# Grouped-query stage of a two-block transformer layer: the projection run to its end first, then scores of two pieces together

## The chip, the cores and the metric

One core of a Trainium2 chip. The metric is device microseconds of one execution, median of the runs.

## What is computed

A hybrid layer (differential attention, gated convolution, memory attention, MLP), then two DiT blocks with modulation. The change lies in the first DiT block's attention: 256 tokens, 16 query heads of 64 over 4 key/value heads, fp32.

```python
qkv = h @ w_qkv
q, k, v = jnp.split(qkv, [Q_WIDTH, Q_WIDTH + KV_WIDTH], axis=-1)
q = apply_rope(rmsnorm(q.reshape(B, T, N_HEADS, HEAD_DIM), q_g), cos, sin)
k = apply_rope(rmsnorm(k.reshape(B, T, N_KV_HEADS, HEAD_DIM), k_g), cos, sin)
...
s = jnp.einsum('bqkgd,bskd->bkgqs', q_blk, k).astype(jnp.float32) * scale
p = jax.nn.softmax(s, axis=-1).astype(v.dtype)
return jnp.einsum('bkgqs,bskd->bqkgd', p, v)
...
return o @ w_o
```

## The kernel before

Every weight is split into a high part (`whi`, cast on ScalarE, L90) and a low part (`wlo`, subtraction on VectorE, L91), so that a product of the large matrices is three TensorE passes (`mm3`, L411 to L414). The class `Weights` keeps the plan of all weights in order of use: it loads 1 MB blocks into three raw buffers from SP's queue, splits them into halves of 128x1024 ahead of use (`pump`), bounded by `W.cap`, and defers each low half a little (`rest`, `get`). The program is written in the order in which each engine executes it; nothing reorders it. Small steps between the large products are put off by ticks: `later(n, f)` runs f n ticks on, and `tick` is called after each unit of weights. Each engine takes its list in order, and waits on semaphores.

The grouped-query stage has three projections of 512 columns: keys and values together, the first half of the queries (heads 0 to 7), the second half. Each is four units of weights, 12 products for each of two token tiles. `gemm_cols_skew` does the first two, `gemm_cols` the third. What comes out is normed and rotated: `evac_kv2` and `evac_q2(n)` take sums of squares (`group_ss`: ScalarE squares, VectorE sums), an inverse root by three Newton steps on GpSimd (`rsqrt`, L276), the rotation on VectorE (`rope`), and turn the result by TensorE (`transpose4`, copied by ScalarE into `kT2`, `qT2`). Queries are turned unnormed; their root `rsq2` enters as the scale of the exponentials.

Then come eight pieces of two heads. Of each: `gq_scores` (four products into two PSUM banks, maxima `nm` and `bias` on VectorE), `gq_exp` (four exponentials with sums, ScalarE), `gq_norm` (reciprocal and division, VectorE), `gq_turn` (eight transposes, one bank copied by ScalarE, one by VectorE), `gq_out` (products with v, then `split_to`: cast `omT` on ScalarE and low half on VectorE). `Rows("o2", 8)` multiplies each output by w_o. `gq_pieces` (L1316) lists which steps of which pieces stand together:

```python
for stage in ((gq_scores, 0, None, 0), (gq_turn, 1, gq_exp, 0), (gq_out, 2, gq_norm, 0)):
```

and `piece` (L1332) runs the next of them, raises `W.cap` by one and pumps. `rows.run` calls it between token tiles for the first two outputs, the loop around it for the rest. At k == 2 the cap falls and two steps of the modulation (`ada`, gate lines L1036) are caught up.

## Time and profile before

| | us |
|---|---|
| median of 3 runs | 1311.92 (1311.72 to 1311.97) |
| the profiled execution | 1312.45 |
| its span, first to last instruction | 1310.7 |
| TensorE products busy in it | 1274.4 (97%) |
| VectorE, ScalarE, GpSimd busy | 931.5, 726.1, 132.5 |

The profile is one execution. Times in its rows are microseconds from the start of the span. PE is TensorE, DVE VectorE, ACT ScalarE, POOL GpSimd; a row names the line, the operation, output and input tiles, and in brackets how long the engine was idle before it and what released it. Rows of TensorE overlap in their ends, so distances are read from start to start.

### The profile page before, as it was taken

The numbers are of one execution on the slowest core, as the hardware profiler recorded it, in microseconds if no ns is written. First come the engines' busy times: TensorE is split into PE (matmuls) and PEld (weight loads), VectorE is DVE, ScalarE is ACT, GpSimd is POOL, SyncE is SP. The second block draws the span as 40 slices with busy tenths as digits, with TensorE's granted clock in tenths as the row PEclk, the third lists the DMA queues.
The fourth block names the chain that finished last, engine by engine and source line by source line (L and its number), as shares of the span: only waits on it lengthen the run. The fifth ranks groups of instructions, "written<-read, shape, count | busy, mean of one in ns | idle before, by whom it ended". The sixth has DMA issues, their size and how long they took to land.

```text
span 1310.7 us, 20502 instructions
## 1 busy us (share of the span) xinstructions
PE 1274.4 (97%) x7891; PEld 1117.4 (85%) x7891; DVE 931.5 (71%) x1435; ACT 726.1 (55%) x1177; POOL 132.5 (10%) x345
## 2 busy tenths in 40 slices
PE   8999999999999999999788999999999999999998
PEld 7788789999998989977556899987889988799896
DVE  5746778856787777777776687776888877764453
ACT  6865666544445645445555666445656543684451
POOL 1222253600001000100400000000000000000000
PEclk9999999999999999999989999999999999999999
DMA  7662344557884888984332588885886765465650
GB/s 249 222 225 98 129 161 162 161 193 238 282 276 153 264 286 292 289 304 157 105 110 65 180 295 283 278 313 164 289 283 221 262 232 194 129 224 191 222 193 33
DMA packets 166990, 275.43 MB, mean 210 GB/s; under 512 B 8444, under 2 KB 95276, under 8 KB 166764
## 3 DMA queue, kind: packets, MB, share of 16 engines
q1 hardware_dynamic: 137292, 219.78, 49.9%
q10 hardware_dynamic: 27808, 50.41, 11.6%
q0 software_dynamic: 1792, 3.92, 1.2%
q8 instruction: 62, 1.02, 0.3%
q14 instruction: 36, 0.29, 0.1%
HBM read 273.04 MB, written 1.05 MB: 209 GB/s over the span
## 4 chain that ended last, share of the span: by engine, by line
PE 72%; DVE 10%; DMA 9%; ACT 5%; POOL 2%; issue 2%; ACTq 0%; SPq 0%; DVEq 0%; POOLq 0%
PE bank L412 12%; PE bank L413 12%; PE bank L414 12%; PE bank L512 9%; PE bank L514 9%; PE bank L513 9%; DMA araw<-in_ada_w_dram 5%; DVE wlo L91 3%; PE bank L462 2%; ACT whi L90 1%; DMA raw<-in_w_mem_kv_dram 1%; DMA raw<-in_attn_w_qkv_dram 1%; ACT p L1288 1%; PE bank L1435 1%; PE bank L453 1%
## 5 line engine op out<-in xcount | busy, mean ns | idle before, releaser
L90 ACT CAST whi<-raw 128x1024 fp32r<-128x1024 f32 x411 | 425.2, 1052 | 265.2 <-PE bank L414 64.5
L91 DVE TENSOR_TENSOR wlo<-raw,whi 128x1024 fp32r<-128x1024 f32 x412 | 495.7, 1219 | 85.3 <-ACT whi L90 83.8
L512 PE MATMUL bank<-hT,whi 128*128 128x256 f32 x1152 | 324.9, 282 | 0.0
L513 PE MATMUL bank<-hT,whi 128*128 128x256 f32 x1152 | 321.5, 279 | 0.0
L514 PE MATMUL bank<-hT,wlo 128*128 128x256 f32 x1152 | 321.4, 279 | 0.0
L512 PEld LDWEIGHTS bank<-hT,whi 128*128 128x128 f32 x1152 | 217.1, 188 | 1.9 <-issue 1.3
L514 PEld LDWEIGHTS bank<-hT,wlo 128*128 128x128 f32 x1152 | 218.2, 189 | 0.0
L513 PEld LDWEIGHTS bank<-hT,whi 128*128 128x128 f32 x1152 | 216.6, 188 | 0.6
L413 PE MATMUL bank<-wlo,act 128*128 128x512 f32 x384 | 150.0, 391 | 2.9 <-DVE wlo L91 2.9
L412 PE MATMUL bank<-whi,act 128*128 128x512 f32 x384 | 150.1, 391 | 0.0
L414 PE MATMUL bank<-whi,act 128*128 128x512 f32 x384 | 149.6, 390 | 0.0
L412 PE MATMUL bank<-whi,hT 128*128 128x512 f32 x308 | 126.4, 410 | 0.8 <-ACT hT L336 0.8
L414 PE MATMUL bank<-whi,hT 128*128 128x512 f32 x308 | 121.1, 393 | 0.0
L413 PE MATMUL bank<-wlo,hT 128*128 128x512 f32 x308 | 120.7, 392 | 0.3 <-DVE wlo L91 0.3
L1036 DVE SCALAR_TENSOR_TENSOR acc<-araw,cond,acc 128x512 f32<-128x512 f32 x128 | 95.4, 746 | 32.3 <-DMA araw<-in_ada_w_dram 32.1
L413 PEld LDWEIGHTS bank<-wlo,act 128*128 128x128 f32 x384 | 72.1, 188 | 18.9 <-DVE wlo L91 4.6
L414 PEld LDWEIGHTS bank<-whi,act 128*128 128x128 f32 x384 | 72.1, 188 | 14.9
L412 PEld LDWEIGHTS bank<-whi,act 128*128 128x128 f32 x384 | 72.1, 188 | 14.5
L412 PEld LDWEIGHTS bank<-whi,hT 128*128 128x128 f32 x308 | 57.9, 188 | 17.5 <-ACT hT L336 4.2
L414 PEld LDWEIGHTS bank<-whi,hT 128*128 128x128 f32 x308 | 57.9, 188 | 13.8 <-DVE hT L325 1.0
L413 PEld LDWEIGHTS bank<-wlo,hT 128*128 128x128 f32 x308 | 58.0, 188 | 12.9 <-DVE wlo L91 0.8
L293 DVE TENSOR_TENSOR act<-s,act 128x512 fp32r<-128x512 f32 x36 | 24.9, 691 | 49.7 <-ACT act L292 49.7
(299 smaller groups left out, 1861.2 us busy)
## 6 DMA issues: line engine op xcount, KB each, us to landing
araw<-in_ada_w_dram ACTq DMA_DIRECT2D x192, 256.0 KB
raw<-in_w_in_dram SPq DMA_DIRECT2D x40, 1024.0 KB
raw<-in_mlp_w_in_dram SPq DMA_DIRECT2D x32, 1024.0 KB
raw<-in_mlp_w_out_dram SPq DMA_DIRECT2D x32, 1024.0 KB
raw<-in_gmlp_w_in_dram SPq DMA_DIRECT2D x24, 1024.0 KB
raw<-in_w_mlp_in_dram SPq DMA_DIRECT2D x16, 1024.0 KB
raw<-in_w_mlp_out_dram SPq DMA_DIRECT2D x16, 1024.0 KB
raw<-in_gmlp_w_out_dram SPq DMA_DIRECT2D x12, 1024.0 KB
```

What stands on the lines that cost most here:

```text
L90: self.nc.scalar.copy(hv, v)
L91: self.rests.append(lambda v=v, hv=hv, lv=lv: self.nc.vector.tensor_sub(lv, v, hv.bitcast(F32)))
L293: V.tensor_sub(lo, src, hi.bitcast(F32))
L412: T.matmul(acc, xh, wh, start=start, stop=False)
L413: T.matmul(acc, xh, wl, start=False, stop=False)
L414: T.matmul(acc, xl, wh, start=False, stop=stop)
L453: T.matmul(acc[c][0], act[0][:, k, 0:P], w[1][:, j, :], start=False, stop=(k == 7))
L462: T.matmul(acc[c][0], act[e][:, k, 0:P], w[0][:, j, :], start=(k + e == 0), stop=False)
L512: T.matmul(acc[:, j], wh[:, k, :], act[0][:, k, :], start=(k == 0), stop=False)
L513: T.matmul(acc[:, j], wh[:, k, :], act[1][:, k, :], start=False, stop=False)
L514: T.matmul(acc[:, j], wl[:, k, :], act[0][:, k, :], start=False, stop=(k == 7))
L1036: V.scalar_tensor_tensor(acc, ada_st.pop(j), cond[:, k:k + 1], acc, op0=ALU.mult, op1=ALU.add)
```

## The change

The change adds `rsqrt_v`, the inverse root as a chain of 11 operations on VectorE, and uses it for the keys and for the first half of the queries; the second half stays on GpSimd. The keys are turned together, one unit of weights later. The third projection runs to its end before q's first half is turned; then the scores and exponentials of pieces 0 and 1 are issued together. The second half of q is squared by ScalarE behind these exponentials and rotated directly from PSUM in two parts, its turn comes after output 0's products, and its sums and root after that. Twelve products of `ones` stand on TensorE behind the first scores. From then on a step issues: scores of piece k+3, products of output k, exponentials of k+3, division of k+2, weight split, output k+1, turn of k+2, split of output k+1.

```diff
--- before.py
+++ after.py
@@ -288,6 +288,19 @@
             E.tensor_scalar(u, u, -1.0, 1.5, op0=ALU.mult, op1=ALU.add)
             E.tensor_mul(y, u, y)
 
+    def rsqrt_v(ss, inv, y):
+
+        shape = list(ss.shape)
+        tag = "x".join(map(str, shape[1:]))
+        h = small.tile(shape, F32, tag=f"rh{tag}", name="rh", bufs=2)
+        u = small.tile(shape, F32, tag=f"ru{tag}", name="ru", bufs=2)
+        V.tensor_scalar(h, ss, -0.5 * inv, -0.5 * EPS, op0=ALU.mult, op1=ALU.add)
+        V.tensor_scalar(y.bitcast(I32), h.bitcast(I32), -0.5, RSQRT_SEED - (1 << 22) - (1 << 30), op0=ALU.mult, op1=ALU.add)
+        for _ in range(3):
+            V.tensor_mul(u, y, y)
+            V.tensor_mul(u, u, h)
+            V.scalar_tensor_tensor(y, u, 1.5, y, op0=ALU.add, op1=ALU.mult)
+
     def split_to(hi, lo, src):
         S.copy(hi, src)
         V.tensor_sub(lo, src, hi.bitcast(F32))
@@ -551,6 +564,8 @@
                     held.append((k, w, act, j))
                     if k < self.nk - 2:
                         self.mm(k, w, act, j, 0)
+                    if self.between:
+                        self.between()
             if k < self.nk - 1:
                 return None
             rate, clock[1] = clock[1], 0.0
@@ -1228,7 +1243,7 @@
         for t in range(NT):
             S.copy(v2[:, t, :], acc[t][:, 256:512])
         kd2 = gp.tile([P, NT, 512], F32, tag="q2", name="kd", bufs=2)
-        rsqrt(group_ss(acc, 4, kd2), 1.0 / 64, rs)
+        rsqrt_v(group_ss(acc, 4, kd2), 1.0 / 64, rs)
         for t in range(NT):
             S.copy(kd2[:, t, 256:512], acc[t][:, 0:256])
 
@@ -1239,26 +1254,36 @@
             kd = kd2[:, t]
             S.copy(kd.rearrange("p (g e d) -> p g e d", e=2, d=64),
                    groups(kn[:, 256:512]).unsqueeze(2).to_broadcast([P, 4, 2, 64]))
-            later(3, lambda: transpose4(kd, kT2[:, :, t * P:(t + 1) * P]))
+            later(4 - t, lambda: transpose4(kd, kT2[:, :, t * P:(t + 1) * P]))
 
         for t in range(NT):
             later(2 + t, lambda t=t: g(t))
+
+    turns = []
 
     def evac_q2(n):
         def f(acc):
             q = gp.tile([P, NT, 512], F32, tag="q2", name="q2", bufs=2)
-            rsqrt(group_ss(acc, 8, q), 1.0 / 64, rsq2[:, :, 8 * n:8 * n + 8])
+            sq = gp.tile([P, NT, 512], F32, tag="sq", name="sq")
+            for t in range(NT):
+                S.activation(sq[:, t], acc[t], AF.Square)
+            ss = small.tile([P, NT, 8], F32, tag="gss8", name="gss", bufs=2)
+
+            def turn(t):
+                transpose4(q[:, t], qT2[:, 4 * n:4 * n + 4, t * P:(t + 1) * P])
+
+            def rest():
+                for t in range(NT):
+                    V.tensor_reduce(ss[:, t], groups(sq[:, t]), axis=AX.X, op=ALU.add)
+                (rsqrt if n else rsqrt_v)(ss, 1.0 / 64, rsq2[:, :, 8 * n:8 * n + 8])
 
             if n:
-                for t in range(NT):
-                    S.copy(q[:, t], acc[t])
-
-            def g(t):
-                rope(q[:, t] if n else acc[t], 8, 0, t, q[:, t])
-                later(3, lambda: transpose4(q[:, t], qT2[:, 4 * n:4 * n + 4, t * P:(t + 1) * P]))
-
+                turns.extend(lambda t=t: turn(t) for t in range(NT))
+                return [lambda t=t: rope(acc[t], 8, 0, t, q[:, t]) for t in range(NT)] + [rest]
             for t in range(NT):
-                later((2 + 2 * t) * n, lambda t=t: g(t))
+                rope(acc[t], 8, 0, t, q[:, t])
+                turns.append(lambda t=t: turn(t))
+            rest()
             if n == 0:
                 S.activation(small.tile([P, 1], F32, tag="exp0", name="exp0", bufs=1), ident[:, 0:1], AF.Exp)
         return f
@@ -1300,7 +1325,7 @@
     def gq_turn(p):
         pT = [attnp.tile([P, 2, 256], F32, tag="pT", name="pT", bufs=4) for _ in range(2)]
         for c in range(2):
-            transpose_p(gq[p][0][c], pT[c].rearrange("p a b -> p (a b)"), on_act=(c == 0))
+            transpose_p(gq[p][0][c], pT[c].rearrange("p a b -> p (a b)"), on_act=(c == 1))
         gq[p] = pT
 
     def gq_out(p):
@@ -1311,43 +1336,80 @@
         for kb in range(2):
             for c in range(2):
                 T.matmul(ps[64 * c:64 * c + 64, 0:256], v2[:, kb, vs], pT[c][:, kb], start=(kb == 0), stop=(kb == 1))
-        split_to(oT2[0][:, p, :], oT2[1][:, p, :], ps[:, 0:256])
-
-    def gq_pieces():
-
-        for j in range(10):
-            for stage in ((gq_scores, 0, None, 0), (gq_turn, 1, gq_exp, 0), (gq_out, 2, gq_norm, 0)):
-                fs = [(f, j - lag) for f, lag in (stage[:2], stage[2:]) if f and 0 <= j - lag < 8]
-                if fs:
-                    yield j - 2 if stage[0] is gq_out else -1, fs
+        return lambda: split_to(oT2[0][:, p, :], oT2[1][:, p, :], ps[:, 0:256])
+
+    step = [0, None]
+
+    def at(lag, f):
+        if 0 <= step[0] - lag < 8:
+            return f(step[0] - lag)
+
+    def gq_first():
+        at(0, gq_scores)
+
+    def gq_mid():
+        at(0, gq_exp)
+        at(1, gq_norm)
+        W.cap += 1
+        W.pump()
+        W.rest(1)
+        step[1] = at(2, gq_out)
+
+    def gq_last():
+        at(1, gq_turn)
+        if step[1]:
+            step[1]()
+        step[0] += 1
+        tick()
 
     rate, clock[1] = clock[1], 0.0
     fillers.append(rope_tables)
     W.cap = W.first("D", ("o2", 0))
     gemm_cols_skew("qkv2", (1024, 0), hT, (evac_kv2, evac_q2(0)), end)
     W.rest()
-    gemm_cols("qkv2", 512, hT, evac_q2(1))
-    pieces = deque(gq_pieces())
-
-    def piece():
-        if pieces:
-            for f, p in pieces.popleft()[1]:
-                f(p)
-        W.cap += 1
-        W.pump()
-        W.rest(1)
+    acc = [bank(ps_a) for _ in range(NT)]
+    for i in range(4):
+        w = W.get("A", ("qkv2", 512))
+        for t in range(NT):
+            col_half(acc, w, hT, i, t)
+        W.done()
         tick()
-
-    rows = Rows("o2", 8, between=piece)
-    for k in range(8):
-        while any(0 <= p <= k for p, _ in pieces):
-            piece()
-        piece()
-        if k == 2:
-            W.cap = 1 << 30
-            while len(ada) > 96:
-                ada.popleft()()
-        end = rows.run(k, [(oT2, k)], residual((0, 0), mods(0, 1)))
+    for f in turns:
+        f()
+    turns.clear()
+    for p in range(2):
+        gq_scores(p)
+    for p in range(2):
+        gq_exp(p)
+    rope_0, rope_1, rest = evac_q2(1)(acc)
+    rope_0()
+    W.cap += 2
+    W.pump()
+    ps = bank(ps_a)
+    for _ in range(12):
+        T.matmul(ps[:, 0:P], ones, ones, start=True, stop=True)
+    gq_norm(0)
+    W.rest(1)
+    gq_turn(0)
+    step[0] = 2
+    rows = Rows("o2", 8, between=gq_mid)
+    for k in range(-1, 8):
+        gq_first()
+        if k < 0:
+            gq_mid()
+        else:
+            if k == 2:
+                W.cap = 1 << 30
+                while len(ada) > 96:
+                    ada.popleft()()
+            end = rows.run(k, [(oT2, k)], residual((0, 0), mods(0, 1)))
+        gq_last()
+        if k == -1:
+            rope_1()
+        elif k == 0:
+            rest()
+            for f in turns:
+                f()
     clock[1] = 0.95
     g_st.close()
     end = mlp("m2i", "m2o", residual((0, 1), mods(1, 0)), end)
```

On VectorE, where the rotation of q's first half ends (`q_7003`, and `q_7000` in the changed program); the `wlo` is the low half of the third projection's last unit. Before:

```order
L1211 TENSOR_TENSOR q_7003<-q_7003,hf 128x512 [waits DVE_49]
L91 TENSOR_TENSOR wlo<-raw,whi 128x1024 [waits PE_49]
L841 TENSOR_REDUCE gss<-q_7112 128x8 [waits Activation_49] x2
L1277 TENSOR_REDUCE nm<-bank 128x2 [waits PE_49] x2
L1279 TENSOR_TENSOR bias<-nm,rsq_6772 128x4 [waits DVE_49,Pool_49]
```

and now (at the dots the last three rows stand twice more, and behind the maxima those of the next piece):

```order
L1226 TENSOR_TENSOR q_7000<-q_7000,hf 128x512 [waits DVE_49]
L1277 TENSOR_REDUCE gss<-sq 128x8 x2
L297 TENSOR_SCALAR rh<-gss 128x16 [waits DVE_49]
L298 TENSOR_SCALAR rsq_6772<-rh 128x2x8 [waits DVE_49]
L300 TENSOR_TENSOR ru<-rsq_6772 128x16 [waits DVE_49]
L301 TENSOR_TENSOR ru<-ru,rh 128x16 [waits DVE_49]
L302 SCALAR_TENSOR_TENSOR rsq_6772<-ru,rsq_6772 128x2x8 [waits DVE_49]
...
L91 TENSOR_TENSOR wlo<-raw,whi 128x1024 [waits PE_49]
L1302 TENSOR_REDUCE nm<-bank 128x2 [waits PE_49] x2
L1304 TENSOR_TENSOR bias<-nm,rsq_6772 128x4 [waits DVE_49]
...
L1224 TENSOR_TENSOR hf<-bank,ropeg 128x256 [waits Activation_49]
```

The root of the first half of q now stands ahead of the low half, and the rotation of the second half (`hf<-bank`) waits for ScalarE behind two pieces' maxima.

On ScalarE, from the copy of the turned q on. Before:

```order
L703 COPY qT_6769<-bank 128x4x128 x2
L840 ACTIVATE q_7112<-bank 128x512 x2
L1254 COPY q_7112<-bank 128x512 x2
L90 CAST whi<-raw 128x1024
L1288 ACTIVATE p,sums<-bank,bias,rsq_6772 128x256 x4
L90 CAST whi<-raw 128x1024 x3
L703 COPY qT_6769<-bank 128x4x128
L791 COPY pT<-bank 128x512
```

and now:

```order
L718 COPY qT_6769<-bank 128x4x128 x2
L1313 ACTIVATE p,sums<-bank,bias,rsq_6772 128x256 x8
L1269 ACTIVATE sq<-bank 128x512 x2
L90 CAST whi<-raw 128x1024 x2
L806 COPY pT<-bank 128x512
L1313 ACTIVATE p,sums<-bank,bias,rsq_6772 128x256 x4
L90 CAST whi<-raw 128x1024
L806 COPY pT<-bank 128x512
```

The squares of the second half (L840, now L1269) moved behind eight exponentials, and its copy out of PSUM is gone; in each later piece the copy `pT` now follows the exponentials and the weight cast.

On VectorE, one later piece. Before:

```order
L1277 TENSOR_REDUCE nm<-bank 128x2 [waits PE_49] x2
L1279 TENSOR_TENSOR bias<-nm,rsq_6772 128x4 [waits DVE_49]
L793 COPY pT<-bank 128x512 [waits PE_49]
L91 TENSOR_TENSOR wlo<-raw,whi 128x1024
L293 TENSOR_TENSOR omT_783<-bank,omT_782 128x256 [waits Activation_49]
L1295 RECIPROCAL rec<-sums 128x4
L1298 TENSOR_SCALAR p<-p,rec 128x256 [waits DVE_49]
L1298 TENSOR_SCALAR p<-p,rec 128x256 x3
```

and now, at piece 4:

```order
L1277 TENSOR_REDUCE gss<-sq 128x8 x2
L1302 TENSOR_REDUCE nm<-bank 128x2 [waits PE_49] x2
L1304 TENSOR_TENSOR bias<-nm,rsq_6772 128x4 [waits DVE_49,Pool_49]
L1320 RECIPROCAL rec<-sums 128x4
L1323 TENSOR_SCALAR p<-p,rec 128x256 [waits DVE_49]
L1323 TENSOR_SCALAR p<-p,rec 128x256 x3
L91 TENSOR_TENSOR wlo<-raw,whi 128x1024
L808 COPY pT<-bank 128x512 [waits PE_49]
L306 TENSOR_TENSOR omT_783<-bank,omT_782 128x256 [waits Activation_49]
```

The division (L1295 and L1298, now L1320 and L1323) moved ahead of the output's low half; the sums of the second q and a wait for GpSimd came in at this piece.

## Rows read from the trace of the kernel before

**Rows 1.** The page, busy tenths of TensorE in 40 slices of the span.

```profile
PE   8999999999999999999788999999999999999998
```

**Rows 2.** The table of stretches: busy time by engine, PEclk granted clock (1.00 is full).

```profile
650.00:655.00 5.00, 2.87 (x12) 1.64 (x10) 4.90 (x11) 3.45 (x5) 3.55 (x9) 0.50 0.08 8
...
700.00:705.00 5.00, 5.00 (x26) 3.44 (x26) 0.79 (x2) 0.90 (x2) 0.00 (x0) 0.66 0.01 3
```

**Rows 3.** The timeline of TensorE around the stage: start, length, line, tiles, [idle before].

```profile
633.01 0.66 PE L698 MATMUL bank<-ident,kd 128*128 128x128 f32 x4 [2.46 <-ACT kd L1240]
...
636.27 0.60 PE L698 MATMUL bank<-ident,kd 128*128 128x128 f32 x4
...
641.62 0.51 PE L413 MATMUL bank<-wlo,hT 128*128 128x512 f32 x1 [0.26 <-DVE wlo L91]
...
644.37 2.00 PE L1274 MATMUL bank<-kT,qT 64*128 64x256 f32 x16
649.56 1.08 PE L698 MATMUL bank<-ident,q 128*128 128x128 f32 x4 [3.19 <-DVE q L1211]
...
699.45 1.50 PE L789 MATMUL bank<-ident,p 128*128 128x128 f32 x8 [2.81 <-DVE p L1298]
```

**Rows 4.** The timeline of VectorE, same columns.

```profile
624.67 2.35 DVE L91 TENSOR_TENSOR wlo<-raw,whi 128x1024 fp32r<-128x1024 f32 x2
630.50 0.43 DVE L1237 TENSOR_TENSOR kn<-kd,rskv 128x256 f32<-128x256 f32 x1 [3.48 <-POOL rskv L289]
...
635.14 1.28 DVE L841 TENSOR_REDUCE gss<-q 128x8 f32<-128x512 f32 x2 [1.24 <-ACT q L840]
636.34 0.75 DVE L1209 TENSOR_TENSOR hf<-bank,ropeg 128x256 f32<-128x256 f32 x2
...
640.34 1.23 DVE L91 TENSOR_TENSOR wlo<-raw,whi 128x1024 fp32r<-128x1024 f32 x1
...
706.30 2.35 DVE L91 TENSOR_TENSOR wlo<-raw,whi 128x1024 fp32r<-128x1024 f32 x2
```

**Rows 5.** The chain of waits through two later pieces: start, length, engine, what.

```profile
678.49 0.93 ACT whi L90
...
682.81 0.67 DVE gate L1036
...
683.93 0.58 ACT pT L791
684.52 2.20 ACT p L1288 x8
...
688.70 1.21 DVE nm L1277 x2
...
690.12 2.29 ACT p L1288 x8
692.42 0.27 ACT omT L292
...
692.71 0.42 DVE omT L293
...
693.25 1.14 DVE p L1298 x4
```

**Rows 6.** The timeline of VectorE in a later stage, its own inverse root.

```profile
981.34 0.17 DVE L283 TENSOR_SCALAR rh<-mv 128x2 f32<-128x2 f32 x1
...
983.93 0.16 DVE L289 TENSOR_TENSOR lnr<-ru,lnr 128x2 f32<-128x2 f32 x1
```

**Rows 7.** The timeline of GpSimd: an undisturbed stretch, then the second half of queries.

```profile
627.16 0.20 POOL L286 TENSOR_TENSOR ru<-rskv 128x8 f32<-128x8 f32 x1
...
630.26 0.20 POOL L289 TENSOR_TENSOR rskv<-ru,rskv 128x8 f32<-128x8 f32 x1
...
645.88 0.20 POOL L283 TENSOR_SCALAR rh<-gss 128x16 f32<-128x16 f32 x1 [3.64 <-DVE gss L841]
...
651.59 0.22 POOL L289 TENSOR_TENSOR rsq<-ru,rsq 128x16 f32<-128x16 f32 x1
```

## The prediction

> **What bounds the kernel now.** I read the page first, then the table of stretches, the timeline of TensorE over the one weak stretch, the timelines of the engines that it waits for, and the chain of waits. TensorE is at 9 tenths almost throughout; the sag in the middle (7, 8, 8) [rows 1] is the grouped-query stage, where the reader sees the granted clock at 0.50 in one stretch and 0.66 in another [rows 2]. Clock 0.50 is the 1.2 GHz level; where the share is 0.66 of 5 us, 3.4 us were spent on it. Outside this stage no row of work moves, so the whole forecast is the date of one event: VectorE's last low half of the attention output. It is followed by a weight's low half at 706.30 [rows 4], and from there TensorE runs without gaps as before. Whatever this date moves by, the end moves by.
>
> Inside the stage two things bind. In the ramp, VectorE: it waits 3.48 us for GpSimd's inverse root of the keys, TensorE behind it 2.46 us for the turned keys [rows 3, 4], and again 3.19 us for the rotated second q [rows 3]. Then a ring per piece of two heads [rows 5]: maxima on VectorE (688.70) and bias, four exponentials on ScalarE (690.12, 2.29), the cast of an output (692.42), its low half on VectorE (692.71), the division of the probabilities (693.25, 1.14), and the next maxima at 694.39. That is 5.70 us; a weight's cast between exponentials and output cast adds 0.93 [rows 5].
>
> **The ramp, step by step.** VectorE finishes the keys' sums at 624.67 [rows 4]. Now it computes the inverse root itself: 11 small operations. A similar chain of 14 elsewhere takes 2.59 us from first to last start, 0.20 each [rows 6], so 2.2: 626.9. Two weight halves, 2.35 [rows 4]: 629.2. From the first key operation until VectorE has the squares of q's first half took 4.64 (630.50 to 635.14) [rows 4]; the same rotation and ScalarE work stands there now: 633.9. The two rotations took 4.00 (636.34 to 640.34) and the sums 1.20 (635.14 to 636.34) [rows 4], now in the other order: 639.1. A second root, 2.2: 641.3. Only then comes the low half of the projection's last unit, begun at 640.34 before.
>
> TensorE needs that low half far earlier. The wait of 2.46 is gone; a unit and four transposes take 3.26 (633.01 to 636.27) [rows 3]. With a further unit ahead of the keys' turn, eight transposes and the third unit, TensorE stands at the fourth at about 636.9. A product began 1.28 after that half (640.34, 641.62) [rows 3, 4]: now 642.6. It stands still 5.7 us. After idle times of 3.19 and 2.81 TensorE came back at half clock (four transposes 1.08 where others took 0.60 and 0.66; the stretch from 700 at 0.66) [rows 2, 3]; I take 3.4 us of half clock here. The rest of the unit took 2.75 (641.62 to 644.37) [rows 3]; with 1.7 lost it is 4.45. The projection ends at **647.05**, against 644.37.
>
> From there, in us behind it. The q transposes (0.8), a copy (0.58 [rows 5]), the first four passes of scores (2.00 for 16 [rows 3]: 0.5) and three hand-overs (one is 0.1: 1.28 from a half's start to its product, less the 1.18 that it lasts [rows 3, 4]) put piece 0's maxima at 2.3. Exponentials start 1.42 later (688.70 to 690.12 [rows 5]), at 3.7; two pieces take 4.4, and piece 1's maxima hide behind them: 8.1. Now a new wait: VectorE's rotation of the second q reads the same bank that ScalarE squares, and the squares stand behind both pieces' exponentials. A square costs about a copy, 0.6: 8.7. The division of piece 0, the turn and everything else stand behind that rotation (half of 4.00): 10.7; division 1.26: 12.0. The twelve idle products follow the scores directly and are over by about 5; nothing holds the clock for the 6 to 7 us until the turn. So I take the turn (8 transposes, begun as soon as half of the division is done) and piece 2's scores (8 passes, 1.0 at full) at half clock: maxima of piece 2 at **14.9**. Before, the ramp took longer from its start, but started earlier.
>
> The Trainium skill, "PSUM — Partial Sum Buffer", section "PSUM bank collisions raise a hardware error", speaks against this placing: reads of one bank by two engines must not overlap, so the wait cannot be dropped, only moved. Could both read at once, the rotation would begin at 5.2 and the forecast be 3.5 lower; no run here shows that.
>
> **The later pieces.** The new order takes the division out of the ring, since it stands before the output's low half and needs only the piece before, and puts one copy of turned probabilities into it: 1.42 + 2.79 (a copy's start to the exponentials' end behind it, 683.93 to 684.52 plus 2.20) + 0.29 + 0.42 [rows 5] = 4.92 instead of 5.70. What is added to single rings:
> - 2 to 3: a cast 0.93, the second rotation 2.0: 7.85, maxima at 22.75.
> - 3 to 4: a cast, the sums of the second q 1.2: 7.05, 29.8.
> - 4 to 5: a cast; and piece 4's bias waits for GpSimd's root, begun only at 29.8. Its 14 operations stood 0.28 apart when undisturbed (627.16 to 630.26, twelve of them) but took 5.9 in the same place before (645.88 to 651.81) [rows 7]. VectorE stands still meanwhile, so I take 4.1, 2.9 more than the maxima's 1.2: 8.75, 38.55.
> - 5 to 6: three casts at once, 2.8 (two of them were earlier before), and the gate step 1.12 (682.81 to 683.93 [rows 5]): 8.85, 47.4.
> - 6 to 7 and 7 to output 5: 4.92 each: 57.2.
> - The end: from 699.45 to 706.30 [rows 3, 4] the same work took 6.85, of which 3.4 at half clock; 5.15 at full. The last copy is no longer covered by products, 0.58 less the early start: 5.5, so **62.7**.
>
> Why GpSimd is quick there has a rule too: the Trainium skill, "GPSIMD Engine Reference", section "Key points", has it share its SBUF interfaces with VectorE and be disturbed by VectorE instructions with two SBUF inputs. By the rule it is the undisturbed pace; by the row of the same place it would be 1.8 more. The trace agrees in so far as the disturbed operations lie beside rotations and weight halves.
>
> **The sum.** 647.05 + 62.7 = 709.75 against 706.30: +3.45 us. The profiled execution took 1312.45 (span 1310.7), 0.5 above the median 1311.92; on that median 1315.4. Costs taken at nothing: the 12 idle products (TensorE is idle there; uncovered 1.3); the roots taken from GpSimd (nobody else waits on it there); DMA, as SP's order is the same and the weights of the next stage wait on the same last low half.
>
> **Bounds.** Full clock in the last unit: 1.7 less; full clock in turn and scores of piece 2: 1.5 less. GpSimd at the old pace: 1.8 more. TensorE waits 2.7 in piece 5 to 6 for its three casts, between the 2.46 that did not lower the clock and the 2.81 that did [rows 3]: 0 or, at half clock, some 3 more, since the turn of piece 5 and the scores of piece 7 then end late.
>
> **Rivals.**
> - *The clock holds in the ramp*, not slower: both idle times leave 2.4 GHz. For it: the idle products aim at that. Against: 5.7 is twice the 2.81. Price −3.2: 1312.2. It decides in the first products after 642.6.
> - *The clock falls in piece 5 to 6*: +3, 1318.4. For it: 2.7 is near 2.81; against, 2.46 passed.
> - *The low half is not late*, faster: if VectorE had the last unit's low half by 636.9, the projection would end at 639.75, 7.3 earlier: 1308.1. Against: it would have to shorten its list from 624.67 by 5.7 of 16.6 us; nothing shrinks so much.
>
> **How the numbers follow.** Forecast 0.52, clock falling later 0.22, clock holding 0.17, half in time 0.09. A measurement of this kernel tells about 0.2%, 2.6 us, from no change: within 1309.3 to 1314.5. The forecast is 0.9 above that; the half clock or a pitch a little off puts 0.14 of its 0.52 inside. Slower 0.38 + 0.22 = 0.60, same 0.14 + 0.17 = 0.31, faster 0.09. The range goes from the clock that holds, 1312.0, to GpSimd's pace and the later fall together, 1320.0; it leaves out the half in time and a little above.
>
> **What would show it.** TensorE's wait of 5 to 6 us for a weight's low half at about 637; VectorE idle some 3.5 us before the second q's rotation, released by ScalarE; half clock in the turn of piece 0; a wait of about 3 us of VectorE for GpSimd at piece 4's bias; rings of 4.9 from piece 6 on. A projection ending before 642, or maxima of piece 4 to 7 in rings under 5.5 each, would make the forecast wrong.

## The result and the profile after

| | before | changed |
|---|---|---|
| median of 8 runs (lowest to highest) | 1311.91 us (1310.88 to 1315.78) | 1319.84 us (1316.54 to 1325.48) |
| profiled execution: time, span | 1312.45, 1310.7 | 1320.18, 1318.4 |
| VectorE's sums of the keys to the low half behind the last output ("the stage") | 624.01 to 706.30: 82.29 | 621.85 to 713.66: 91.81 |

The ratio is 1.0061, 95% interval 1.0046 to 1.0076: the change is slower by 7.9 us (0.6%), where 3.5 were forecast. In the profiled execution the stage comes 2.16 us earlier than before and takes 9.5 us longer; behind it the rows of both kernels read alike. Over the profiles of this document the stage starts anywhere between 617.6 and 624.5, though nothing is edited ahead of it, so a difference of a microsecond or two between times says little by itself. On the page, TensorE's sag has grown from 7, 8, 8 tenths [rows 1] to 6, 8, 8:

```profile
PE   9999999999999999999688999999999999999998
```

The table of stretches of the changed kernel (columns: length, busy time of PE, weight loads, VectorE, ScalarE, GpSimd, granted clock, DMA) shows half clock at three places, where [rows 2] had two:

```profile
635.00:640.00 5.00, 0.00 (x0) 0.00 (x0) 4.60 (x15) 0.00 (x0) 0.00 (x0) 0.86 0.00 0
640.00:645.00 5.00, 4.61 (x11) 3.64 (x12) 0.34 (x1) 0.00 (x0) 0.00 (x0) 0.50 0.58 210
...
655.00:660.00 5.00, 2.86 (x12) 2.40 (x14) 4.44 (x10) 2.35 (x3) 0.00 (x0) 0.57 0.00 0
...
690.00:695.00 5.00, 2.28 (x9) 1.47 (x8) 4.13 (x6) 3.64 (x6) 0.00 (x0) 0.83 0.29 54
695.00:700.00 5.00, 5.00 (x16) 2.59 (x14) 2.47 (x8) 2.30 (x8) 0.00 (x0) 0.50 0.40 155
```

The timeline of TensorE (start, length, line, tiles, [idle before it and who ended that]) answers to [rows 3]:

```profile
640.39 0.80 PE L426 MATMUL bank<-wlo,hT 128*128 128x512 f32 x1 [5.57 <-DVE wlo L91]
...
645.25 1.15 PE L713 MATMUL bank<-ident,q 128*128 128x128 f32 x8
...
657.14 1.94 PE L804 MATMUL bank<-ident,p 128*128 128x128 f32 x8 [5.57 <-DVE p L1323]
659.01 2.08 PE L1299 MATMUL bank<-kT,qT 64*128 64x256 f32 x8
...
693.42 2.07 PE L1299 MATMUL bank<-kT,qT 64*128 64x256 f32 x6 [2.61 <-ACT pT L806]
...
698.28 1.95 PE L1338 MATMUL bank<-pT,v 128*64 128x256 f32 x8
```

The wait of 2.46 for the turned keys is gone; in its place stands 5.57 for the last unit's low half, then 5.57 for piece 0's division, and in piece 6's scores 2.61 for a copy of ScalarE. Behind each of the three it runs at half clock (eight passes of scores take 2.08 where 16 had taken 2.00 [rows 3]). VectorE, who is waited for, answers to [rows 4]:

```profile
621.85 0.75 DVE L856 TENSOR_REDUCE gss<-kd 128x4 f32<-128x256 f32 x2 [0.55 <-ACT kd L855]
...
639.12 1.22 DVE L91 TENSOR_TENSOR wlo<-raw,whi 128x1024 fp32r<-128x1024 f32 x1
647.86 1.29 DVE L1302 TENSOR_REDUCE nm<-bank 128x2 f32<-128x512 f32 x2 [7.52 <-PE bank L1299]
...
654.44 0.76 DVE L1224 TENSOR_TENSOR hf<-bank,ropeg 128x256 f32<-128x256 f32 x2 [3.69 <-ACT sq L1269]
...
661.12 1.29 DVE L1302 TENSOR_REDUCE nm<-bank 128x2 f32<-128x512 f32 x2 [1.60 <-PE bank L1299]
...
680.43 0.16 DVE L1304 TENSOR_TENSOR bias<-nm,rsq 128x4 f32<-128x4 f32 x1 [2.78 <-POOL rsq L289]
...
694.70 1.53 DVE L1302 TENSOR_REDUCE nm<-bank 128x2 f32<-128x512 f32 x2 [0.38 <-PE bank L1299]
...
700.86 0.69 DVE L808 COPY pT<-bank 128x512 f32<-128x512 f32 x1 [3.17 <-PE bank L804]
...
702.59 1.28 DVE L1302 TENSOR_REDUCE nm<-bank 128x2 f32<-128x512 f32 x2
...
713.66 2.35 DVE L91 TENSOR_TENSOR wlo<-raw,whi 128x1024 fp32r<-128x1024 f32 x2
```

Read it as a list of dates. The low half of the last unit starts behind both rotations, the sums and the root, at 639.12. The rotation of the second q waits 3.69 for ScalarE's squares. Piece 4's bias waits 2.78 for GpSimd's root. From piece 6's maxima (694.70) to piece 7's (702.59) it takes 7.89, though an undisturbed ring, from 702.59 to the low half and reciprocal at 707.69, takes 5.10 (5.70 before [rows 5]). On ScalarE's timeline stands what holds piece 6's scores: three weight casts in a row ahead of the copy at 692.77 that frees their second bank.

```profile
689.95 2.94 ACT L90 CAST whi<-raw 128x1024 fp32r<-128x1024 f32 x3
692.77 0.60 ACT L806 COPY pT<-bank 128x512 f32<-128x512 f32 x1
```

### The profile page after: what moved, and what is told of

Read it like the earlier page. It is cut to its first block, busy times and chain, and to the rows that moved or that the text cites. A ratio compares the mean times of both kernels' runs of the same rounds, so it can differ in the third digit from the quotient of the medians.

```text
span 1318.4 us, 20543 instructions
## 1 busy us (share of the span) xinstructions
PE 1284.8 (97%) x7915; PEld 1124.6 (85%) x7915; DVE 936.0 (71%) x1457; ACT 724.2 (55%) x1175; POOL 121.4 (9%) x317
## 3 DMA queue, kind: packets, MB, share of 16 engines
HBM read 273.04 MB, written 1.05 MB: 208 GB/s over the span
## 4 chain that ended last, share of the span: by engine, by line
PE 82%; DVE 7%; DMA 4%; ACT 3%; POOL 2%; issue 1%; ACTq 0%; DVEq 0%; POOLq 0%
PE bank L425 13%; PE bank L426 13%; PE bank L427 13%; PE bank L525 11%; PE bank L526 11%; PE bank L527 11%; DMA araw<-in_ada_w_dram 2%; PE bank L475 2%; DVE wlo L91 2%; ACT p L1313 1%; PE bank L1497 1%; PE bank L466 1%; PE bank L323 1%; ACT whi L90 1%; DMA raw<-in_w_mem_kv_dram 1%
## 5 line engine op out<-in xcount | busy, mean ns | idle before, releaser
L1051 DVE SCALAR_TENSOR_TENSOR gate<-araw,cond,gate 128x512 f32<-128x512 f32 x64 | 47.8, 748 | 15.9 <-DMA araw<-in_ada_w_dram 15.7
```

What stands on the lines that cost most here:

```text
L1051: V.scalar_tensor_tensor(acc, ada_st.pop(j), cond[:, k:k + 1], acc, op0=ALU.mult, op1=ALU.add)
```

## The experiments

Twelve runs: e10 is the changed kernel once more, and the other eleven are made from it by the edit shown. Times are medians; the ratio is against the kernel before, run beside it. The stage of one profiled execution is cut at VectorE's maxima (nm) of pieces 0, 2, 6 and 7.

| run | keys' sums to nm 0 | 0 to 2 | 2 to 6 | 6 to 7 | 7 to end | stage | median | ratio (95%) |
|---|---|---|---|---|---|---|---|---|
| changed | 26.01 | 13.26 | 33.58 | 7.89 | 11.07 | 91.81 | 1319.84 | 1.0061 (1.0046 to 1.0076) |
| e10 the same again | 26.17 | 13.25 | 33.58 | 7.93 | 11.06 | 91.99 | 1319.57 | 1.0053 (1.0035 to 1.0071) |
| e1 low half first | 17.81 | 13.27 | 33.91 | 5.26 | 11.07 | 81.32 | 1311.62 | 0.9992 (0.9981 to 1.0002) |
| e2 squares first | 26.47 | 8.78 | 33.73 | 6.77 | 11.05 | 86.80 | 1315.93 | 1.0028 (1.0017 to 1.0040) |
| e3 root early | 25.13 | 13.26 | 32.25 | 7.98 | 11.05 | 89.67 | 1316.95 | 1.0038 (1.0025 to 1.0051) |
| e4 hold clock | 25.31 | 13.27 | 33.15 | 5.27 | 11.07 | 88.07 | 1319.85 | 1.0045 (1.0033 to 1.0058) |
| e5 casts spread | 26.26 | 13.27 | 31.05 | 5.94 | 13.43 | 89.95 | 1319.15 | 1.0057 (1.0042 to 1.0071) |
| e6 no idle products | 26.06 | 13.26 | 33.58 | 7.91 | 11.07 | 91.88 | 1319.05 | 1.0069 (1.0052 to 1.0085) |
| e7 division back | 26.46 | 13.26 | 38.00 | 6.93 | 12.51 | 97.16 | 1326.35 | 1.0119 (1.0102 to 1.0135) |
| e8 e1+e2+e3+e5 | 17.98 | 8.77 | 30.06 | 7.93 | 11.90 | 76.64 | 1306.19 | 0.9960 (0.9946 to 0.9974) |
| e9 e8 and idle products | 17.98 | 8.78 | 30.22 | 5.95 | 13.48 | 76.41 | 1305.54 | 0.9951 (0.9933 to 0.9969) |
| e11 casts behind | 25.94 | 13.26 | 31.04 | 5.86 | 10.96 | 87.06 | 1317.05 | 1.0039 (1.0023 to 1.0054) |
| e12 e1+e2+e3+e11 | 17.82 | 8.99 | 29.72 | 5.85 | 10.95 | 73.33 | 1301.97 | 0.9932 (0.9914 to 0.9951) |

Median less stage lies between 1227 and 1230.5 in every line but e4's (1231.8; the kernel before has 1229.6): to within these 3.5 us, what an edit does, it does in this stage. The stage is that of one execution, and the executions of one kernel are not alike in their clock: e9's nine range from 0.993 of full clock over the whole span (1310.28 us) to 1.000 (1299.81 us). A column tells where the time went in the execution shown, and the median what the edit is worth.

**e1: the late low half.** In the evacuation of q's first half, ahead of the rotations:

```diff
+            W.rest()
             for t in range(NT):
                 rope(acc[t], 8, 0, t, q[:, t])
```

> VectorE does the low half of the projection's last unit before the rotations of q's first half, not behind them and their inverse root; nothing else moves. Theory (the late low half is the largest term): TensorE's wait of 5.57 us ahead of the last unit and the half clock in that unit go. VectorE is then the ramp's bound: rotations, sums and root end 1.2 us later than in the changed kernel, at about 640.4, and piece 0's maxima start there instead of at 647.86: 7.5 us less, 1312.3 us for the changed kernel's 1319.8. Rival A (the root on VectorE is the cost, wherever the low half stands): the maxima start no earlier than 646, at most 2 us less. Rival B (it is only the half clock): the wait moves behind the unit, and only the 1.9 us that the unit takes longer at half clock are won.

Measured: 8.2 us less in the median, 8.2 less to piece 0's maxima. VectorE's timeline:

```profile
630.85 1.22 DVE L91 TENSOR_TENSOR wlo<-raw,whi 128x1024 fp32r<-128x1024 f32 x1
...
640.19 1.29 DVE L1303 TENSOR_REDUCE nm<-bank 128x2 f32<-128x512 f32 x2 [0.45 <-PE bank L1300]
```

The low half cost nothing where it was put: VectorE had stood still 1.24 us there, waiting for squares. That is why 8.2 came back and not the 7.5 expected. Rivals A and B fall; with this one line the change as a whole is level with the kernel before. The stage of e1's profile is 10.5 shorter, more than the 8.2, because ring 6 to 7 took 5.26: the clock fell a piece earlier, in piece 5's scores, behind waits of no more than 0.70, and was back at 1.00 in piece 6, though the same three casts stand there:

```profile
676.82 2.07 PE L1300 MATMUL bank<-kT,qT 64*128 64x256 f32 x6 [0.42 <-DVE pT L808]
...
686.56 1.13 PE L1300 MATMUL bank<-kT,qT 64*128 64x256 f32 x6 [1.61 <-ACT pT L806]
```

**e2: the squares behind the exponentials.**

```diff
+    rope_0, rope_1, rest = evac_q2(1)(acc)
     for p in range(2):
         gq_exp(p)
-    rope_0, rope_1, rest = evac_q2(1)(acc)
     rope_0()
```

> ScalarE squares the second half of q before the eight exponentials of pieces 0 and 1, not behind them; nothing else moves. ScalarE stood idle 2.37 us ahead of the exponentials, and the two squares take 1.1. Theory (the rotation waits for the squares, and piece 2 stands behind the rotation): VectorE's wait of 3.69 us ahead of the rotation goes, the turn of piece 0 starts 3.7 us earlier: 1316.1 us for 1319.8; 1315 if TensorE, idle 4 us less, keeps its clock there. Rival A (the exponentials themselves bind piece 2, as ScalarE's list is the same length): the division of piece 0 needs only piece 0's sums, so piece 2's own exponentials would have to wait for ScalarE; then under 1 us less. Rival B (two weight casts behind the squares bind): 0.

Measured: 3.9 less in the median. VectorE rotates right behind piece 1's bias (653.75), and TensorE's turn comes after 1.79 us of idleness instead of 5.57, at full clock:

```profile
656.45 1.24 PE L804 MATMUL bank<-ident,p 128*128 128x128 f32 x8 [1.79 <-DVE p L1323]
657.62 1.13 PE L1299 MATMUL bank<-kT,qT 64*128 64x256 f32 x8
```

From piece 0 to 2 it is 4.48 less: 3.7 of the wait and 0.8 of half clock. ScalarE's list is as long as it was; only its order cost.

The two reads of the bank are still in turn. The Trainium skill, "PSUM — Partial Sum Buffer", section "PSUM bank collisions raise a hardware error", has two engines' reads of one bank kept apart, and the rows agree in that the rotation of a bank does not begin before its square is done (squares from 653.78, rotation at 654.44 in the changed kernel; from 650.06 and at 653.75 in e2); what the order of the two costs is a matter of what stands ahead of the first reader.

**e3: GpSimd's root a piece earlier.**

```diff
         if k == -1:
             rope_1()
+            rest()
         elif k == 0:
-            rest()
             for f in turns:
```

> The sums of the second q's squares and GpSimd's root stand one piece earlier, right behind the second rotation instead of behind the output of the step after; nothing else moves. Theory (the wait for GpSimd is on the path): the wait of 2.78 us ahead of piece 4's bias goes, as the root has a ring of 7 us to be done in; the sums, 1.27, only change rings: 2.8 less, 1317.0 us for 1319.8. Rival A (GpSimd takes 6 us or more beside VectorE's division and low half, as the same root took 5.9 in the kernel before): still done in time, also 2.8 less, but with a root of 6 us instead of 4.05. Rival B (ScalarE or TensorE end ring 4 to 5 anyway): under 1 us less.

Measured: 2.9 less in the median, the theory's 2.8, but that is in part luck: the rings of its profile gave back only 1.3 (2 to 6: 32.25 for 33.58). The wait for GpSimd is gone; in ring 3 to 4, from which the sums were taken, VectorE now waits 1.30 for scores of TensorE, which stands behind the second q's turns and their copies. Rival B is half right. GpSimd's timeline, beside VectorE's:

```profile
670.85 0.20 POOL L288 TENSOR_SCALAR ru<-ru 128x16 f32<-128x16 f32 x1
671.14 1.27 POOL L289 TENSOR_TENSOR rsq<-ru,rsq 128x16 f32<-128x16 f32 x1
```

```profile
669.91 1.29 DVE L1323 TENSOR_SCALAR p<-p,rec 128x256 f32<-128x256 f32 x4
671.12 1.21 DVE L91 TENSOR_TENSOR wlo<-raw,whi 128x1024 fp32r<-128x1024 f32 x1
...
675.63 0.69 DVE L1302 TENSOR_REDUCE nm<-bank 128x2 f32<-128x512 f32 x1 [1.30 <-PE bank L1299]
```

One GpSimd operation of 0.22 lasts 1.27, just as long as the weight's low half beside it, and the root takes 5.1 instead of 4.05; beside maxima and division it kept its pitch of 0.3. The division did not come off free: it took 1.29 there for 1.14 without GpSimd beside it, and 1.76 beside the root in the kernel before. The Trainium skill, "GPSIMD Engine Reference", section "Key points", names as contending with GpSimd the VectorE instructions with two SBUF inputs, or in a mode that takes two ports. The rows agree for the low half (raw and high half, both in SBUF); which case the division is, no run here shows.

**e10 and e4: does the clock fall as a rule, and what is it worth?** e10 has no edit.

> The changed kernel once more, without an edit, beside the run above: a second profile of it. Theory (the clock falls in piece 5 to 6 as a rule, because three casts keep TensorE waiting): again a wait of some 2.6 us between the two banks of piece 6's scores, a stretch at or near 0.50 between 690 and 705, ring 6 to 7 of 7 to 8 us, and a stage of 91 to 92 us; 1319.8 us. Rival (the fall was an accident of the profiled execution): a ring 6 to 7 near 5.1 and a stage of 88 to 89.

The second profile repeats the first to 0.2 us in every column:

```profile
694.53 2.07 PE L1299 MATMUL bank<-kT,qT 64*128 64x256 f32 x6 [2.61 <-ACT pT L806]
```

So the fall is no accident of the first profile. It need not come in every execution, though: over the whole span, two of e10's nine have a granted clock of 0.994, the others 0.990 to 0.993, and these two are the fastest (1314.71 and 1315.11 us). No trace shows where they kept it.

e4 fills that gap in `gq_scores`:

```diff
+        if p == 6:
+            for _ in range(10):
+                T.matmul(pss[0][:, 0, 0:P], ones, ones, start=True, stop=True)
```

> Ten idle products of the matrix of ones stand ahead of piece 6's scores, in a bank that these overwrite, where TensorE waited 2.61 us between the first and the second bank of the scores; the three weight casts stay where they are. Theory (the half clock costs by itself): the scores' six passes, 2.07 before, take about 1.1 and the output, the turn and the next scores likewise; ring 5 to 6 gets 0.9 shorter, ring 6 to 7 goes from 7.89 to 5.1: 3.7 less, 1316.1 us for 1319.8. Rival A (the three casts cost, and the clock only follows): 0. Rival B (the idle products end late, behind the copy that frees the second bank): up to 0.5 more.

In the profile the theory holds: the wait shrinks to 0.19, the six passes take 1.13, ring 6 to 7 takes 5.27 and ring 5 to 6 9.03, together 3.1 less. The stage is 3.7 shorter, as expected, but 0.7 of that lies ahead of piece 0's maxima, where the edit does nothing.

```profile
685.17 2.50 PE L1298 MATMUL bank<-ones 128*128 128x128 f32 x20
...
688.48 1.13 PE L1302 MATMUL bank<-kT,qT 64*128 64x256 f32 x6 [0.19 <-ACT pT L806]
```

The median does not follow and stands at rival A's figure, 0, though the profile speaks against rival A: 1319.85, with runs from 1311.45 (the profiled one, whose stage also began 4.3 us earlier than the changed kernel's) to 1320.96. By the ratios it is 0.1 to 0.2% below the changed kernel, with overlapping intervals. In most of these runs the clock is not what is missing: over the whole span seven of the twelve runs have 0.994 or 0.995, where the changed kernel's eight have 0.989 to 0.992, and four of these seven still took 1319.8 us or more. Their time went elsewhere; where, no trace shows. So the idle products show what the half clock costs inside a profile, and not that they are worth adding.

**e5 and e11: the casts.** e5 lifts the limit on casts at the last product row (`k == 7` for `k == 2`); e11 lifts it at the same step, behind that step's copies:

```diff
             if k == 2:
-                W.cap = 1 << 30
                 while len(ada) > 96:
...
         gq_last()
+        if k == 2:
+            W.cap = 1 << 30
+            W.pump()
```

> The limit on weight casts ahead is lifted at the last product row instead of at the third: instead of three casts at once in ring 5 to 6, one stands in each of the rings 5 to 6, 6 to 7 and 7 to output 5. The same casts, spread. Theory (what costs is TensorE's wait of 2.61 us and the half clock that follows it): the wait falls under 1 us, the clock stays at 1.00 from piece 5 to the end; ring 5 to 6 loses two casts and the slow scores (9.5 to about 6.8), ring 6 to 7 is 5.1 plus a cast (7.89 to 6.05), the next gets a cast, 0.95: some 3.5 us less, 1316.3 us for 1319.8. Rival A (only ScalarE's time counts): two casts less, twice one more: 0. Rival B (the clock falls in these rings for another reason, the short gaps of each ring): still 0.50 in some stretch from 690 to 705, and within 1 us of 0.

> The limit on casts is lifted at the same step, but two of the three casts are issued behind that step's copy of turned probabilities and output cast, where ScalarE stood idle 2.88 us ahead of piece 6's exponentials; their two low halves move into ring 6 to 7. Theory (the casts' place keeps TensorE waiting, and the clock falls by that wait): ring 5 to 6 about 6.9 us for 9.5, ring 6 to 7 about 6.3 for 7.89, as VectorE's list of that ring is 6.2 with both low halves: 4.2 us less in the stage, 1315.5 us for 1319.8. Rival A (the clock then falls in the last stretch instead, as where the casts were spread: 7.49 for 5.97): 2.7 less, 1317. Rival B (as with the idle products ahead of piece 6's scores, the stage gets shorter and the median does not): within 1 us of 1319.8.

e5's rings came as priced (5 to 6 6.93, 6 to 7 5.94, the next 5.94), and then 1.5 were lost again: a cast now stands ahead of the copy and output cast that TensorE waits for in the last ring, and the clock fell there.

```profile
705.48 0.79 PE L425 MATMUL bank<-whi,omT 128*128 128x512 f32 x1 [2.13 <-ACT omT L305]
```

The stage is 1.9 shorter for the 3.5 expected, and the median moved by 0.7: rival B's figure, though the fall stands behind 705 and not ahead of it. Spreading moves the fall. e11 is the cleaner one. The two casts lie in time in which ScalarE was idle, ahead of piece 6's exponentials:

```profile
690.93 0.60 ACT L806 COPY pT<-bank 128x512 f32<-128x512 f32 x1
691.40 0.40 ACT L305 CAST omT<-bank 128x256 fp32r<-128x256 f32 x1
691.67 2.02 ACT L90 CAST whi<-raw 128x1024 fp32r<-128x1024 f32 x2
693.75 0.57 ACT L1313 ACTIVATE p<-bank,bias,rsq 128x256 f32<-128x256 f32 x1
```

The stage is 4.75 shorter (4.2 expected), the clock is 1.00 in every stretch from 665 on, and the median is 2.8 lower. Rival A, the fall in the last stretch, is refuted in the profile, though the median lies at its figure.

**e6: the twelve idle products** of the ramp, left out.

```diff
-    ps = bank(ps_a)
-    for _ in range(12):
-        T.matmul(ps[:, 0:P], ones, ones, start=True, stop=True)
```

> The twelve idle products behind the scores of pieces 0 and 1 are left out; nothing that the output needs. Theory (TensorE is idle there anyway and the clock has fallen by the turn either way): maxima of piece 2 at the same distance from the start, 0 within 1 us, 1319.8 us. Rival A (they keep the clock, or let it come back sooner, in pieces 2 and 3): 1 to 3 us more. Rival B (they stand in the way of the turn): 1 us less or more than that.

The stage is the same to 0.1 us: they cost nothing and hold nothing, as TensorE rests another 5.57 us behind them.

**e7: the ring's new order, undone.** The division leaves `gq_mid` and stands in `gq_last` behind the low half; piece 1's stands ahead of the loop.

```diff
         at(0, gq_exp)
-        at(1, gq_norm)
...
             step[1]()
+        at(0, gq_norm)
```

> One part undone: the division of a piece's probabilities stands again behind the output's low half of the same step, in the ring, as in the kernel before, instead of in the shadow of the next exponentials. All other parts of the change stay. Theory (the new order of the ring is a gain of the change, hidden by the losses): an undisturbed ring goes from 5.10 us to 5.10 plus a reciprocal and a division, 1.26, 6.36; six rings: 6 to 7.5 us more, about 1326.5 us for 1319.8. Rival A (the division was never the bound, the rings are held by casts, gate and clock): under 2 us more. Rival B (a longer ring lets TensorE rest longer, and the clock falls in the later rings too): over 9 us more.

Measured: 6.5 more. VectorE waits 2.34 for the output's cast, and reciprocal and division follow in the ring:

```profile
668.97 0.42 DVE L306 TENSOR_TENSOR omT<-bank,omT 128x256 fp32r<-128x256 f32 x1 [2.34 <-ACT omT L305]
669.31 0.17 DVE L1320 RECIPROCAL rec<-sums 128x4 f32<-128x4 f32 x1
669.51 1.14 DVE L1323 TENSOR_SCALAR p<-p,rec 128x256 f32<-128x256 f32 x4
```

The rings 2 to 3, 3 to 4 and 4 to 5 are 1.27, 1.05 and 1.31 longer, as the 1.26 of the theory. Behind piece 5 the price is blurred, as the clock fell at other places than in the changed kernel (ring 6 to 7 is 0.96 shorter, the end 1.44 longer); the whole stage is 5.4 longer. So the change holds a real gain of 5 to 6.5 us, which its losses hide.

**e8, e9, e12: the repairs together.** e8 is the edits of e1, e2, e3 and e5, e12 those of e1, e2, e3 and e11. e9 adds to e8:

```diff
-    for _ in range(12):
+    for _ in range(20):
         T.matmul(ps[:, 0:P], ones, ones, start=True, stop=True)
...
+        for _ in range(3 if p > 2 else 0):
+            T.matmul(pss[0][:, 0, 0:P], ones, ones, start=True, stop=True)
```

> All four repairs at once: the low half ahead of the rotations, the squares ahead of the exponentials, the second root one piece earlier, the casts spread. Theory (the losses stand one behind the other in the same chain, so the gains add): 8.2 us as measured for the low half, 3.7 to 4.4 for the squares, 1.3 to 2.8 for the root (in its profile only half of the wait was won back), some 3 for the casts: 16 to 18 less, 1302 to 1304 us, 8 to 10 below the kernel before. Rival A (with the ramp short, another engine ends it: VectorE's list of rotations, sums and root, or ScalarE's casts): 1306 to 1309. Rival B (the clock falls elsewhere instead): 1308 or more, with a stretch of 0.50 in the rings.

> The four repairs as in the run before, and idle products in TensorE's gaps: twenty instead of twelve behind the scores of pieces 0 and 1, three ahead of the scores of each of the pieces 3 to 7, in the bank that those scores overwrite. Theory (what is left of the loss is half clock: in the four repairs' profile piece 2's turn and scores ran slow, 0.88 and 0.78 in the stretches, and piece 6's at 0.50): both stretches return to 1.00, the ring of piece 6 goes from 7.93 us to about 5.9, the ramp loses 1: 3 us less than the four repairs, 1303 us for 1306.2. Rival A (three products, 0.75 us, stand in the path of the scores as often as not): 0 to 3 more. Rival B (the clock falls all the same, in another ring): within 1 us of 1306.2, with a stretch of 0.50 between pieces 2 and 7.

> The repairs of the low half, the squares and the second root, with the casts placed as in the run above instead of spread over three rings. Theory (the spread casts lie in the ring, one cast of 0.95 in each of the rings to piece 7 and to output 5; here they lie in ScalarE's idle time): the ring behind piece 6 may lose 0.8 to the two low halves, the last gets 0.95 shorter: 1 us less than the four repairs' 1306.2, 1305. Rival A (half clock in piece 6, 2 us in the four repairs' profile, does not come as TensorE rests less): 1303. Rival B (the clock falls elsewhere): 1306 to 1307.

e8 is 5 us faster than the kernel before and 13.7 faster than the changed one, where 16 to 18 were expected: the root and the spread casts gave less than in the sum, and in piece 6 the clock fell (7.93 from piece 6 to 7) in the profiled execution, which has the lowest clock of the six (0.994 over the span, the others 0.996 to 0.998). The time is rival A's, the mechanism rival B's: the ramp was as short as in e1 and e2 (17.98 and 8.77). e9 fills the gaps: the ramp and piece 6 run at 1.00, and the clock falls in the last stretch instead, where nothing was filled:

```profile
645.00:650.00 5.00, 3.79 (x30) 2.92 (x30) 4.06 (x9) 4.23 (x11) 0.00 (x0) 1.00 0.00 0
...
690.00:695.00 5.00, 3.62 (x12) 2.24 (x14) 1.89 (x7) 1.33 (x3) 0.00 (x0) 0.68 0.00 0
```

The times are the same, as rival B had it, with the fall in a later ring than it named. In the ramp the full clock brought nothing at all (8.78 for 8.77), since VectorE's list ended last there. e12, with the casts in ScalarE's idle time, beats both kernels: 1301.97 us, 0.68% below the kernel before and 3 below the 1305 expected, since piece 6 kept its clock (rival A, 1303). In its profile the clock is below 1.00 only around piece 2's scores (0.66 in the stretch from 645). The single runs add up: 8.2 to piece 0 (e1), 4.5 to piece 2 (e2), 1.3 (e3) and 4.7 (e11) make 18.7; the stage of e12 is 18.5 shorter than that of the changed kernel. On its page one slice is left of TensorE's sag, at 8, where three stood at 7, 8, 8 [rows 1]:

```profile
PE   9999999999999999999989999999999999999998
```

## Why the prediction was right, and where it was short

The direction and the mechanism held: slower, because the last unit's low half comes late, and because new waits stand in the ramp. The forecast's dates, set to this execution's 2.16 earlier start, against the rows:

- *The last low half at 641.3* (639.14 here): 639.12. Two roots of 11 operations on VectorE at 0.20 to 0.21 each, the reordered rotations and sums, all as summed.
- *TensorE stands still 5.7 us, and comes back at half clock*: 5.57, clock 0.50. The projection ends at 645.25 for 644.89. The rival in which the clock holds falls here. e1 prices the step at 8.2; the rival "half in time" had it at 7.3.
- *The rotation waits for the squares, 8.7 behind the projection's end*: 9.19, with the wait of 3.69; e2. *Half clock in the turn and in piece 2's scores*: yes, 1.94 and 2.08. *Maxima of piece 2 at 14.9*: 15.87. Nearly one more, from small steps taken too short: half of it up to the rotation (2.61 for 2.3 to piece 0's maxima is the largest part), half behind the division (3.4 for 2.9 to piece 2's maxima).
- *Rings to piece 5: 7.85, 7.05, 8.75*: 7.92, 7.33, 8.83. GpSimd's root took 4.05 at its undisturbed pace (4.1 taken), since VectorE stood still; the 5.9 of [rows 7] did not come back.
- *Ring 5 to 6, 8.85; 6 to 7, 4.92*: 9.50 and **7.89**. This is the step that failed.
- *7 to output 5, 4.92; the end 5.5*: 5.10 and 5.97.

The failed step reads: "TensorE waits 2.7 in piece 5 to 6 for its three casts, between the 2.46 that did not lower the clock and the 2.81 that did [rows 3]: 0 or, at half clock, some 3 more". The wait was well seen, 2.61; the 0 was the wrong choice. The clock fell, in both profiles of the changed kernel, and rings 5 to 6 and 6 to 7 were 3.6 longer than forecast. With the ramp's missing 1.3 (0.4 in the projection, 1.0 to piece 2) and 1.1 in the other rings and the end, that is the whole difference between 3.45 and the 9.5 of the profile. The rival that had this fall gave 1318.4, 1.4 below the measured median. The stated range, 1312.0 to 1320.0, reached so far up because it took in GpSimd's old pace (1.8) together with the fall (some 3). GpSimd's old pace did not come back, and the small terms, 2.4, took its place: that 1319.84 lies just inside is partly luck. In the medians, which differ by 7.9, the fall weighs less than in the profile: e11, which takes the fall and its cause away, gives back 2.8, and e4, which takes the fall alone, nothing that can be told. Why e4's median does not follow its profile is open, and so is what made the clock fall: e11 shows that it does not fall when the three casts stand elsewhere, but in e1 they stand where they stood and piece 6 keeps its clock.

What was costed at nothing was nothing: the idle products (e6) and, as far as executions that differ by some 2 us outside the stage can tell, everything outside the stage.

## What to carry to other kernels

When an operation is put into a queue earlier, look what now stands behind it and who starves: a single weight's low half behind two rotations and a root cost 8 us, and one added line won them back. A list that is no longer than before can still cost by its order (squares behind exponentials, casts ahead of a copy); the place to put such work is the idle time that the timeline shows ahead of a wait. Filling TensorE's gaps with idle products mends the clock in the stretch filled, and is worth something only if TensorE is what ends that stretch; even there (e4) no gain in the median was shown.

## What the runs showed of the hardware that was not expected

- The length of one wait did not tell whether the clock falls. It stayed at 1.00 behind 2.46 [rows 3] and fell behind 2.61, behind 2.13 (e5), and behind the 1.79 ahead of piece 0's turn in e8 and e12, while the same 1.79 at the same place in e2 left it at 1.00. A limit between 2.46 and 2.81, on which the prediction leaned, does not hold. In e8 it even fell in piece 6's scores behind waits of 0.70 and 0.38, and in e12 the same two waits left it at 1.00 (e8's row first, then e12's):

```profile
679.48 2.07 PE L1300 MATMUL bank<-kT,qT 64*128 64x256 f32 x6 [0.38 <-DVE pT L808]
...
676.77 1.13 PE L1300 MATMUL bank<-kT,qT 64*128 64x256 f32 x6 [0.38 <-DVE pT L808]
```

- The fall moves: with one gap mended, half clock turned up at another (piece 6 in e8, the last stretch in e5 and e9). The later rings were free of it in e4, e11 and e12, in one profile each; what decides it there, no run shows.
- One VectorE operation with two SBUF inputs stopped a GpSimd operation for its whole length: 1.27 for 0.22 (e3).
